# Gates of an expert layer: index selection in 16-bit floats, four heads at a time

## The chip, the cores and the metric

The kernel runs on one core of a Trainium2 chip, in one launch. The metric is device time in microseconds (us) from start to end of an execution. The engines are TensorE (PE, with PEld its weight loads), VectorE (DVE), ScalarE (ACT), GpSimd (POOL) and the DMA queues, of which SP's carries nearly all direct transfers and POOL's the indirect gathers.

## The reference, cut to what matters

The reference is a block with a gated linear recurrence, a convolution, an expert layer, and then two attention layers with their MLPs, all over 512 tokens of width 1024. The change is in the expert layer:

```python
def peer_layer(h, w_q, sub_keys, u_tab, v_tab):          # 512 tokens, 8 heads, 128 x 128 experts
    q = (hf @ w_q).reshape(T, 8, 2, 128)
    s = jnp.einsum('thpd,hpnd->thpn', q, sub_keys)       # two lists of 128 scores for each head
    sc, idx = lax.top_k(s, 16)
    cand = (sc[:, :, 0, :, None] + sc[:, :, 1, None, :]).reshape(T, 8, 256)
    cidx = (idx[:, :, 0, :, None] * 128 + idx[:, :, 1, None, :]).reshape(T, 8, 256)
    top_sc, pos = lax.top_k(cand, 16)
    eidx = jnp.take_along_axis(cidx, pos, axis=-1)       # 16 experts for each head and token
    gate = jax.nn.softmax(top_sc, axis=-1)
    act = jax.nn.gelu(jnp.einsum('thkd,td->thk', u_tab[eidx], hf), approximate=False)
    return jnp.einsum('thk,thkd->td', gate * act, v_tab[eidx])
```

The last two lines run in blocks of 128 tokens in the reference.

## The kernel before

The 512 tokens are four blocks of 128, one token to a partition. `stage_p` treats them in two ways. Block 0 gathers: for each of its 128 (head, choice) slots an indirect DMA fetches one row of `peer_u` for each token (`gu`, 512 KB, four buffers), VectorE makes the dot product with the token (`gather_dots`, L662), and later the rows of `peer_v` (`gv`) are fetched and summed with their weights (`gather_sums`, L677 and L679). Blocks 1 to 3 are dense: all 16384 experts are multiplied with 384 tokens, `peer_u` in 32 chunks of four units of 512 KB (`unit`: load `raw` in SP's queue, ScalarE rounds it to `whi` in L103, VectorE makes the rest `wlo` in L104; then three products for each step, L121 to L123), with GELU into `at`, which goes to DRAM. The gates become a dense array G (128 x 128 experts for each token): VectorE makes one-hot rows of 16 tokens at a time from the two indices (L735 to L738, 16-bit), TensorE multiplies them (L743, L744), ScalarE evicts into the tile `G` (32 tokens, one buffer), and SP writes it to DRAM as `g_d` (L749), four times for a block, 12 in all. The second part (`p2`) reads `at` and `g_d` back (`gt`), multiplies them to `w` (L600), splits `w` (ScalarE and L113) and multiplies it with `peer_v` (L610 to L612), chunk by chunk; it can't begin before all of G is there, since each chunk of `gt` takes a slice from all 12 writes.

The indices come from `route`. After the top-16 of the scores, `gates` runs once for each block, all on VectorE but for one exponential: 50 candidate sums for a head, their top 16 with positions `pos`, the softmax `g`, and then the selection, which turns a position among the candidates into the two indices. The candidates lie in 16 segments; `pcst[:, 0]` holds the segments' starts, `pcst[:, 1]` the lengths. For each head, over 16 choices x 16 segments: M is 1 where the position is at or behind the start; the row sum of M times D (differences of the first indices) is the first index `iv`; the row sum of M times the lengths, taken from the position, is the place in the segment `bb`; M is then 1 at that place, and the row sum of M times the second indices is `jv`. These are nine operations in a row, on one pair of tiles M and Q.

Block 0's indices become `eidx`, and only then the gathers can start. Blocks 1 to 3 go through `gates_t` (transposes on TensorE, 16-bit copies) to the one-hot rows. The tiles of `gates` have one buffer each.

The order of work on each engine is made by the framework's planner when the kernel is built: it goes through the program with a priority for each instruction (program order, and a higher one for the loads and splits of `unit`) and a simulated time, and takes what is ready. Each engine then executes its list in order. So `wlo`, dots, one-hot rows and gates are mixed on VectorE, and an edit of durations can change the order of all lists.

Of the kernel before, what the change touches and what calls it, by code (L numbers as in the profile page):

```python
# [9 lines left out]
F32 = mybir.dt.float32  # L10
F32R = mybir.dt.float32r
F16 = mybir.dt.float16
# [3 lines left out]
ALU = mybir.AluOpType  # L16
AX = mybir.AxisListType
# [3 lines left out]
P = 128  # L21
# [31 lines left out]
class Kern:  # L53
# [628 lines left out]
    def route(self, pq, X, g_d, gather):  # L682
        nc, tc, A = self.nc, self.tc, self.A
        with self.pool("p_rt") as pt:
            iota = pt.tile([P, P], F32, name="iota")
            nc.sync.dma_start(out=iota, in_=A["iota"])
            self.iota16 = iota[:, 0:16]
            pcst = pt.tile([P, 2, 16], F32, name="pcst")
            nc.sync.dma_start(out=pcst, in_=A["peer_cst"])
            v16 = [pt.tile([P, 16, 16], F32, name=f"v16_{b}") for b in range(4)]  # L690
            i16 = [pt.tile([P, 16, 16], U32, name=f"i16_{b}") for b in range(4)]
            with self.pool("p_route") as pr:
# [14 lines left out]
            with self.pool("p_gates") as pr:  # L707
# [8 lines left out]
                g, iv, jv = self.gates(pr, v16[0], i16[0], pcst)  # L716
# [7 lines left out]
                for b in range(1, 4):  # L724
                    gT, iT, jT = self.gates_t(pr, pq, *self.gates(pr, v16[b], i16[b], pcst))
                    for hf in range(4):
                        G = pr.tile([P, P, 32], F32, tag="G", name="G", bufs=1)
                        for c in range(2):
# [10 lines left out]
                            for t4 in range(4):  # L739
                                ps = pq.tile([P, T], F32, tag="G", name="Gp").rearrange("p (t i) -> p t i", t=4)  # L740
                                for tt in range(4):
# [5 lines left out]
                                    out=G[:, :, u0:u0 + 4], in_=ps.rearrange("p t i -> p i t"), func=AF.Copy, scale=2.0 ** -15)  # L747
# [11 lines left out]
    def gates(self, pr, v16, i16, pcst):  # L759
        nc = self.nc  # L760

        def t(tag, shape, dt=F32, bufs=1):
            return pr.tile([P] + shape, dt, tag=tag, name=tag, bufs=bufs)
        fi = t("fi", [16, 16])
        nc.vector.tensor_copy(out=fi, in_=i16)
        vv = v16.rearrange("p (h s) a -> p h s a", s=2)
        ff = fi.rearrange("p (h s) a -> p h s a", s=2)
        cand = t("cand", [8, NCAND])
        cand2 = t("cand2", [8, NCAND])
        for a in range(16):  # L770
            s0, n = STARTS[a], SEG[a]
            nc.vector.tensor_tensor(
                cand[:, :, s0:s0 + n], vv[:, :, 1, 0:n], vv[:, :, 0, a:a + 1].to_broadcast([P, 8, n]), ALU.add)
        top = t("top", [8, 16])
        pos = t("pos", [8, 16], U32)
        for h in range(8):
            self.top16(top[:, h], pos[:, h], cand[:, h], cand2[:, h])
        g = t("g", [8, 16])
        ssum = t("ssum", [8, 1])
        nc.vector.tensor_tensor(g, top, top[:, :, 0:1].to_broadcast([P, 8, 16]), ALU.subtract)  # L780
        nc.scalar.activation(out=g, in_=g, func=AF.Exp)
        nc.vector.tensor_reduce(out=ssum, in_=g, axis=AX.X, op=ALU.add)
        nc.vector.reciprocal(out=ssum, in_=ssum)
        nc.vector.tensor_tensor(g, g, ssum.to_broadcast([P, 8, 16]), ALU.mult)
        pf = t("pf", [8, 16])
        nc.vector.tensor_copy(out=pf, in_=pos)

        D = t("D", [8, 16])
        nc.vector.tensor_copy(out=D[:, :, 0:1], in_=ff[:, :, 0, 0:1])
        nc.vector.tensor_tensor(D[:, :, 1:16], ff[:, :, 0, 1:16], ff[:, :, 0, 0:15], ALU.subtract)  # L790
        iv, jv, bb = t("iv", [8, 16]), t("jv", [8, 16]), t("bb", [8, 16])
        M, Q = t("M", [16, 16]), t("Q", [16, 16])
        for h in range(8):
            def row(x):
                return x.unsqueeze(1).to_broadcast([P, 16, 16])

            def col(x):
                return x.unsqueeze(2).to_broadcast([P, 16, 16])
            nc.vector.tensor_tensor(M, col(pf[:, h]), row(pcst[:, 0]), ALU.is_ge)
            nc.vector.tensor_tensor(Q, M, row(D[:, h]), ALU.mult)  # L800
            nc.vector.tensor_reduce(out=iv[:, h], in_=Q, axis=AX.X, op=ALU.add)
            nc.vector.tensor_tensor(Q, M, row(pcst[:, 1]), ALU.mult)
            nc.vector.tensor_reduce(out=bb[:, h], in_=Q, axis=AX.X, op=ALU.add)
            nc.vector.tensor_tensor(bb[:, h], pf[:, h], bb[:, h], ALU.subtract)
            nc.vector.tensor_tensor(M, col(bb[:, h]), row(self.iota16), ALU.is_equal)
            nc.vector.tensor_tensor(Q, M, row(ff[:, h, 1]), ALU.mult)
            nc.vector.tensor_reduce(out=jv[:, h], in_=Q, axis=AX.X, op=ALU.add)
        return g, iv, jv

    def gates_t(self, pr, pq, g, iv, jv):  # L810
# [564 lines left out]
def pack(I):  # L1375
    I = {k: np.asarray(v) for k, v in I.items()}
    D = {}
    D["x"] = np.ascontiguousarray(I["x"][0].T.reshape(KD, P, T).transpose(1, 0, 2))
    vec = [
# [5 lines left out]
    ]  # L1385
    D["vec"] = np.ascontiguousarray(np.concatenate(vec, axis=1))
    D["c"] = I["c"]
# [50 lines left out]
```

## Time and profile before

| | us |
|---|---|
| median of 3 runs | 3200.18 (3192.09 to 3202.19) |
| the profiled execution, its own time | 3207.16 |
| its span, first to last instruction | 3205.2 |
| PE busy | 3065.3 (96%) |
| DVE busy | 2249.6 (70%) |
| ACT busy | 1243.2 (39%) |
| POOL busy | 415.1 (13%) |

The mean granted clock of TensorE is 0.979. `route` and the first part of the expert layer lie between about 640 and 1350 us of the span, the second part ends at about 1940. Times inside the span are counted from its first instruction. The shares are means over all stages; the rows further down are from the expert layer alone.

### The profile page before, as it was taken

The page shows a single profiled execution, that of the slowest core. Times are in us where ns is not written, and L with a number is a line of the kernel's source. Part 1 is how long each engine was busy: PE and PEld are TensorE (multiplying, and loading weights), DVE is VectorE, ACT ScalarE, POOL GpSimd, SP SyncE. Part 2 cuts the span into 40 slices and gives each one's busy share as a digit, 9 for nine tenths or more (in the row PEclk, how much of TensorE's full clock was granted, in tenths as well). Part 3 has the DMA queues.
Part 4 walks back from the last instruction along what each step waited for, and adds up shares of the span by engine and source line. Part 5 has one row for each costly group of instructions (what it writes and reads, how often), then busy time and mean ns, then how long its engine had stood idle before and what let it go on. Part 6 is the DMA issues. An engine that isn't in the chain of part 4 may idle for free.

```text
span 3205.2 us, 40593 instructions
## 1 busy us (share of the span) xinstructions
PE 3065.3 (96%) x15313; PEld 2592.2 (81%) x15313; DVE 2249.6 (70%) x4020; ACT 1243.2 (39%) x1963; POOL 415.1 (13%) x328
## 2 busy tenths in 40 slices
PE   5999999899999999798988999999999999999998
PEld 4778878789999999687777788678888877778886
DVE  7989977699899998577777655545544457554443
ACT  3257762334334343332222334553222245532221
POOL 0000000000334332034444101000000000000000
PEclk9999999999999999899999999999999999999999
DMA  6452227434899998798998753222333333133332
GB/s 219 143 168 72 68 85 250 153 98 158 303 336 362 325 361 332 249 361 321 353 335 321 284 170 93 61 66 81 105 99 93 110 92 96 51 96 97 97 99 72
DMA packets 199827, 579.71 MB, mean 181 GB/s; under 512 B 18288, under 2 KB 72448, under 8 KB 198096
## 3 DMA queue, kind: packets, MB, share of 16 engines
q1 hardware_dynamic: 159424, 431.36, 40.5%
q0 software_dynamic: 39776, 144.97, 12.1%
q8 instruction: 120, 1.97, 0.3%
q10 hardware_dynamic: 432, 0.80, 0.1%
q14 instruction: 75, 0.61, 0.1%
HBM read 525.34 MB, written 62.21 MB: 183 GB/s over the span
## 4 chain that ended last, share of the span: by engine, by line
PE 70%; DVE 10%; DMA 9%; issue 6%; ACT 2%; POOL 2%; SPq 0%; POOLq 0%; DVEq 0%; ACTq 0%
PE g L121 17%; PE g L122 17%; PE g L123 17%; DMA gv<-in_peer_v,eidx 3%; DVE wlo L104 2%; DMA raw<-in_peer_v 2%; DMA gu<-in_peer_ur,eidx 2%; DVE gu L662 2%; PE S L1245 1%; PE g L610 1%; PE ac L610 1%; PE g L611 1%; PE g L612 1%; PE ac L611 1%; PE ac L612 1%
## 5 line engine op out<-in xcount | busy, mean ns | idle before, releaser
L103 ACT CAST whi<-raw 128x1024 fp32r<-128x1024 f32 (+1 forms) x553 | 575.8, 1049 | 1203.5 <-PE g L122 667.1
L121 PE MATMUL g<-xh,whi 128*128 128x512 f32 (+1 forms) x2408 | 892.3, 372 | 17.8 <-ACT xh L112 8.9
L123 PE MATMUL g<-xh,wlo 128*128 128x512 f32 (+1 forms) x2408 | 891.4, 371 | 6.6 <-DVE wlo L104 6.6
L122 PE MATMUL g<-xl,whi 128*128 128x512 f32 (+1 forms) x2408 | 894.4, 372 | 3.4 <-DVE xl L113 3.4
L104 DVE TENSOR_TENSOR wlo<-raw,whi 128x1024 fp32r<-128x1024 f32 (+1 forms) x553 | 675.3, 1224 | 194.7 <-ACT whi L103 191.1
L121 PEld LDWEIGHTS g<-xh,whi 128*128 128x128 f32 x2408 | 456.2, 190 | 81.0 <-ACT xh L112 9.4
L123 PEld LDWEIGHTS g<-xh,wlo 128*128 128x128 f32 x2408 | 456.0, 189 | 63.7 <-DVE wlo L104 8.9
L122 PEld LDWEIGHTS g<-xl,whi 128*128 128x128 f32 x2408 | 456.0, 189 | 61.6 <-DVE xl L113 5.6
L653 POOL DMA_INDIRECT gv<-in_peer_v,eidx x128 | 197.0, 1539 | 352.7 <-DVE yt L679 240.7
L653 POOL DMA_INDIRECT gu<-in_peer_ur,eidx x128 | 161.6, 1263 | 475.8 <-DVE ga L662 226.6
L610 PE MATMUL g<-whi,wph 128*128 128x512 f32 x384 | 156.1, 408 | 52.6 <-ACT whi L103 37.2
L122 PE MATMUL g<-ml,whi 128*128 128x512 f32 x512 | 199.2, 389 | 0.0
L121 PE MATMUL g<-mh,whi 128*128 128x512 f32 x512 | 199.2, 389 | 0.0
L123 PE MATMUL g<-mh,wlo 128*128 128x512 f32 x512 | 199.2, 389 | 0.0
L188 POOL TENSOR_TENSOR tr_r<-tr_v,mhalf 128x4 f32<-128x4 f32 x15 | 16.4, 1094 | 1275.7 <-DVE tr_v L187 1275.7
L927 DVE TENSOR_TENSOR h<-g,h 128x512 f32<-128x512 f32 x64 | 44.3, 692 | 194.1 <-PE g L123 194.1
L679 DVE SCALAR_TENSOR_TENSOR yt<-gv,ga,yt 128x1024 f32<-128x1024 f32 x127 | 163.0, 1284 | 11.6 <-DMA gv<-in_peer_v,eidx 10.8
L327 DVE SCALAR_TENSOR_TENSOR s<-glu,vec,s 128x512 f32<-128x512 f32 x232 | 165.4, 752 | 0.1
L662 DVE CUSTOM_DVE_ANT_0 gu<-gu,xt 128x1024 f32<-128x1024 f32 x128 | 155.3, 1219 | 13.8 <-DMA gu<-in_peer_ur,eidx 13.7
L610 PE MATMUL ac<-whi,wph 128*128 128x512 f32 x384 | 157.5, 411 | 0.0
L611 PE MATMUL ac<-whi,wpl 128*128 128x512 f32 x384 | 156.6, 408 | 0.0
L611 PE MATMUL g<-whi,wpl 128*128 128x512 f32 x384 | 155.4, 405 | 0.0
(446 smaller groups left out, 4616.6 us busy)
## 6 DMA issues: line engine op xcount, KB each, us to landing
raw<-in_peer_u SPq DMA_DIRECT2D x128, 512.0 KB, 6.0
raw<-in_peer_v SPq DMA_DIRECT2D x128, 512.0 KB, 8.6
raw<-in_mlp_in SPq DMA_DIRECT2D x64, 512.0 KB, 3.6
raw<-in_mlp_out SPq DMA_DIRECT2D x64, 512.0 KB, 3.6
raw<-in_w_in SPq DMA_DIRECT2D x56, 512.0 KB, 3.6
g_d<-G SPq DMA_DIRECT2D x12, 2048.0 KB, 11.1
gt<-g_d SPq DMA_DIRECT2D x32, 768.0 KB, 8.8
act_d<-at SPq DMA_DIRECT2D x31, 768.0 KB, 7.3
```

Of the source, the lines that this page charges most:

```text
L103: nc.scalar.copy(out=hi[:, :n], in_=raw[:, :n])
L104: nc.vector.tensor_sub(out=lo[:, :n], in0=raw[:, :n], in1=hi[:, :n].bitcast(F32))
L121: nc.tensor.matmul(ps, wh, xh, start=start, stop=False)
L122: nc.tensor.matmul(ps, wh, xl, start=False, stop=False)
L123: nc.tensor.matmul(ps, wl, xh, start=False, stop=stop)
L327: nc.vector.scalar_tensor_tensor(o, glu[n][:, j:j + T], self.v("conv_w", n * 31 + j), acc, ALU.mult, ALU.add)
L610: nc.tensor.matmul(ps, wh[:, i], hi[:, s], start=first, stop=False)
L611: nc.tensor.matmul(ps, wl[:, i], hi[:, s], start=False, stop=False)
L612: nc.tensor.matmul(ps, wh[:, i], lo[:, s], start=False, stop=last)
L653: self.nc.gpsimd.indirect_dma_start(out=t, out_offset=None, in_=tab, in_offset=bass.IndirectOffsetOnAxis(ap=self.eidx[:, s:s + 1], axis=0))
L662: nc.vector.tensor_tensor_reduce(out=u, in0=u, in1=self.xt, scale=1.0, scalar=0.0, op0=ALU.mult, op1=ALU.add, accum_out=self.ga[:, s:s + 1])
L679: nc.vector.scalar_tensor_tensor(self.yt, v, self.ga[:, s:s + 1], self.yt, ALU.mult, ALU.add)
```

## The change

The selection works on four heads at a time (64 rows of choices in place of 16), so that nine operations for each of eight heads become nine for each of two halves. M, Q, the positions, D, the second indices, the place and the constants are 16-bit floats (all values are whole numbers up to 128); the sums `iv`, `bb`, `jv` stay fp32. Where a value repeats along a row it is stored twice in a row (`pf`, `b2`), so that the innermost dimension of every operand is a pair or longer. New are the copy `f1` for each block and two copies of constants at the start.

```diff
-            self.iota16 = iota[:, 0:16]
-            pcst = pt.tile([P, 2, 16], F32, name="pcst")
-            nc.sync.dma_start(out=pcst, in_=A["peer_cst"])
+            pc32 = pt.tile([P, 2, 16], F32, name="pc32")
+            nc.sync.dma_start(out=pc32, in_=A["peer_cst"])
+            pcst = pt.tile([P, 3, 16], F16, name="pcst")
+            nc.vector.tensor_copy(out=pcst[:, 0:2], in_=pc32)
+            nc.vector.tensor_copy(out=pcst[:, 2], in_=iota[:, 0:16])
...
-        pf = t("pf", [8, 16])
-        nc.vector.tensor_copy(out=pf, in_=pos)
-
-        D = t("D", [8, 16])
+
+
+        pf = t("pf", [8, 16, 2], F16)
+        nc.vector.tensor_copy(out=pf, in_=pos.unsqueeze(3).to_broadcast([P, 8, 16, 2]))
+
+        D = t("D", [8, 16], F16)
...
+        f1 = t("f1", [8, 16], F16)
+        nc.vector.tensor_copy(out=f1, in_=ff[:, :, 1])
         iv, jv, bb = t("iv", [8, 16]), t("jv", [8, 16]), t("bb", [8, 16])
-        M, Q = t("M", [16, 16]), t("Q", [16, 16])
-        for h in range(8):
...
+        b2 = t("b2", [8, 16, 2], F16)
+        M, Q = t("M", [64, 16], F16), t("Q", [64, 16], F16)
+
+        def pairs(x):
+            return x.rearrange("p n (a two) -> p n a two", two=2)
+
+        def col(x, h4):
+            return x[:, h4].rearrange("p h k two -> p (h k) two").unsqueeze(2).to_broadcast([P, 64, 8, 2])
+
+        def row(x):
+            return x.rearrange("p (a two) -> p a two", two=2).unsqueeze(1).to_broadcast([P, 64, 8, 2])
+
+        def heads(x):
+            return x.rearrange("p (h k) a -> p h k a", k=16)
+
+        def hrow(x, h4):
+            return x[:, h4].unsqueeze(2).to_broadcast([P, 4, 16, 16])
+
+        def total(out, h4):
+            nc.vector.tensor_reduce(out=out[:, h4], in_=heads(Q), axis=AX.X, op=ALU.add)
+        for h4 in (slice(0, 4), slice(4, 8)):
+            nc.vector.tensor_tensor(pairs(M), col(pf, h4), row(pcst[:, 0]), ALU.is_ge)
+            nc.vector.tensor_tensor(heads(Q), heads(M), hrow(D, h4), ALU.mult)
+            total(iv, h4)
+            nc.vector.tensor_tensor(pairs(Q), pairs(M), row(pcst[:, 1]), ALU.mult)
+            total(bb, h4)
+            nc.vector.tensor_tensor(b2[:, h4], pf[:, h4], bb[:, h4].unsqueeze(3).to_broadcast([P, 4, 16, 2]), ALU.subtract)
+            nc.vector.tensor_tensor(pairs(M), col(b2, h4), row(pcst[:, 2]), ALU.is_equal)
+            nc.vector.tensor_tensor(heads(Q), heads(M), hrow(f1, h4), ALU.mult)
+            total(jv, h4)
```

## Rows read from the trace of the kernel before

**Rows 1.** Stretches: length, busy time (instructions) of PE, PEld, DVE, ACT, POOL; PEclk, DMA share, GB/s.
```profile
818.00:1060.00 242.00, 241.08 (x1557) 237.61 (x1556) 229.35 (x429) 98.01 (x146) 93.24 (x76) 1.00 0.94 347
1060.00:1233.00 173.00, 166.79 (x1092) 161.33 (x1091) 163.74 (x262) 67.25 (x105) 59.94 (x48) 0.97 0.94 347
1233.00:1321.00 88.00, 85.39 (x617) 82.35 (x616) 68.27 (x70) 40.28 (x66) 13.84 (x9) 0.98 0.77 270
1321.00:1348.00 27.00, 5.64 (x49) 5.37 (x49) 4.67 (x5) 6.50 (x10) 0.00 (x0) 0.65 0.63 231
...
1400.00:1800.00 400.00, 361.50 (x1478) 290.92 (x1477) 297.49 (x233) 114.75 (x104) 164.72 (x107) 0.94 0.90 329
```

**Rows 2.** Chain of waits, 1314 to 1356 us: start, length, what.
```profile
1317.55 8.77 DMA g_d<-G
...
1333.00 6.27 DMA g_d<-G
1339.34 4.90 DMA gt<-g_d
1344.33 1.77 DVE w L600
...
1347.64 1.65 PE g L610 x3
...
1350.57 0.43 PE g L611
...
1355.07 0.23 PE g L612
```

**Rows 3.** Timeline of ACT at the last `peer_u` unit: start, length, instruction.
```profile
1320.88 0.48 ACT L581 ACTIVATE at<-g 128x384 f32<-128x384 f32 x1
```

**Rows 4.** Timeline of SP's queue: writes of `g_d`, last of block 1 to first of block 3.
```profile
1047.11 0.87 SPq L749 DMA_DIRECT2D g_d<-G  x1
...
1119.15 0.33 SPq L749 DMA_DIRECT2D g_d<-G  x1
...
1201.35 0.85 SPq L749 DMA_DIRECT2D g_d<-G  x1
...
1269.17 0.42 SPq L749 DMA_DIRECT2D g_d<-G  x1
```

**Rows 5.** Timeline of DVE: steps among other work; last steps of blocks 2 and 3.
```profile
842.69 1.21 DVE L104 TENSOR_TENSOR wlo<-raw,whi 128x1024 fp32r<-128x1024 f32 x1
843.83 0.41 DVE L801 TENSOR_REDUCE iv<-Q 128x16 f32<-128x256 f32 x1
844.16 1.21 DVE L662 CUSTOM_DVE_ANT_0 gu<-gu,xt 128x1024 f32<-128x1024 f32 x1
...
1074.81 0.42 DVE L807 TENSOR_REDUCE jv<-Q 128x16 f32<-128x256 f32 x1
...
1229.11 0.41 DVE L807 TENSOR_REDUCE jv<-Q 128x16 f32<-128x256 f32 x1
```

**Rows 6.** Groups on DVE, 700 to 1480 us: instruction and count | busy us, mean ns | idle before.
```profile
L104 DVE TENSOR_TENSOR wlo<-raw,whi 128x1024 fp32r<-128x1024 f32 x159 | 194.4, 1225 | 30.1 <-ACT whi L103 29.6 <-PE Gp L744 0.4
...
L735 DVE TENSOR_TENSOR oj<-io,jT 128x2048 f16<-128x2048 f16 x24 | 29.0, 1220 | 0.0
...
L799 DVE TENSOR_TENSOR M<-pf,pcst 128x256 f32<-128x256 f32 x32 | 13.9, 433 | 0.0
...
L802 DVE TENSOR_TENSOR Q<-M,pcst 128x256 f32<-128x256 f32 x32 | 13.4, 419 | 0.4
L803 DVE TENSOR_REDUCE bb<-Q 128x16 f32<-128x256 f32 x32 | 13.3, 414 | 0.5
...
L804 DVE TENSOR_TENSOR bb<-pf,bb 128x16 f32<-128x16 f32 x32 | 5.5, 171 | 0.4
```

**Rows 7.** Instructions on the tile `gv`: duration min/median/max ns, first and last start.
```profile
L679 DVE SCALAR_TENSOR_TENSOR yt<-gv,ga,yt x127: 1269/1280/1322, 1351.6 to 1814.7; 128x1024 f32<-128x1024 f32 x127
```

**Rows 8.** Waits of POOL, 740 to 1262 us: total us, times, longest.
```profile
POOL gu L653 <- DVE ga L662: 226.6, 97, 7.3
```

More of the change, by code (lines that the diff above doesn't have):

```diff
@@ L791, in gates @@
+        nc.vector.tensor_copy(out=f1, in_=ff[:, :, 1])
         iv, jv, bb = t("iv", [8, 16]), t("jv", [8, 16]), t("bb", [8, 16])
-        M, Q = t("M", [16, 16]), t("Q", [16, 16])
-        for h in range(8):
[L794 to L807, printed above, removed]
+        b2 = t("b2", [8, 16, 2], F16)
```

## The prediction

> **What bounds the kernel now.** I read four views in this order: the stretches, to see which engine is full where the gates run; the chain of waits at the end of that stage; the queues and timelines, to see what makes that end late; the groups of instructions, for the prices.
>
> The stretches [rows 1] show the expert layer's first part. From 818 to 1321 us three things are full at once: TensorE (241.08 of 242 us, 166.79 of 173, 85.39 of 88), VectorE (95% until 1233 us, 78% after) and the DMA engines (share 0.94, then 0.77). TensorE does the dense products with `peer_u` and, in between, the small one-hot products that build G. It can't go faster, so taking work from VectorE is worth only what TensorE now waits for. In the three stretches that is 0.92 + 6.21 + 2.61 = 9.7 us. The large hole comes next: from 1321 to 1348 us TensorE works 5.64 of 27 us, and the granted clock is 0.65 on the mean: after some 6 us of standing still it goes from the upper of its two levels (2.4 GHz) to the lower (1.2 GHz).
>
> The chain of waits [rows 2] says who makes this hole. The last `peer_u` unit is evicted at 1320.88 us [rows 3], but the last quarter of G of the last token block waits until the quarter before it has left its only buffer (1317.55 + 8.77 us); then it is built, goes to DRAM (6.27), comes back as `gt` (4.90), is multiplied and split, and TensorE starts the second part at 1347.64. Its first products take 0.43 us each, against 0.23 at 1355 us, back at the upper level.
>
> Why is G late? The `g_d` writes in the SP queue [rows 4]: the four of block 2 go from 1119.15 to 1201.35, 27 us apart, but between the last of block 1 (1047.11) and the first of block 2 there are 72 us, and between the last of block 2 and the first of block 3 (1269.17) 68. The holes are gates: those of block 2 end at 1074.81 and those of block 3 at 1229.11 [rows 5], each about 28 us after the previous block's last `g_d`. And the gates are slow because each of their operations depends on the one before: the same rows show the planner putting a `wlo` of 1.21 us or a dot (L662) of 1.21 us between one operation and the next. From 842.69 to 844.16 a `wlo` and one selection step of 0.41 us together take a turn of 1.5 us, and a dot follows. A block has 72 such steps, 9 for each of 8 heads.
>
> **The change, part by part.** Durations are from [rows 6].
>
> Removed, for each head: five operations of 128x256 at 419 to 433 ns (L799, L800, L802, L805, L806), three reductions at 414, one subtraction at 171. That is 2.11 + 1.24 + 0.17 = 3.53 us; times 8 heads, times 4 blocks: 113 us.
>
> Added, for each half of four heads: five operations of 128x1024 in 16 bits. L735, whose operands are in pairs and 16 bits wide as here, does 2048 elements in the 1220 ns that L104 needs for 1024 in fp32. So 1024 in pairs cost what 512 cost in fp32; between 256 (420 ns) and 1024 (1225 ns) the slope is 1.05 ns an element, so 0.69 us. Three reductions of 1024: no row has one in 16 bits. Bounds: 1.22 us at the fp32 rate (a reduction of 256 costs 414 ns, as much as a product of 256), 0.69 at the pairs' rate; I take 1.22, because the reductions of before are the nearest rows. The subtraction now writes 128 values with one fp32 input: 0.29 by the same slope. Sum 5 x 0.69 + 3 x 1.22 + 0.29 = 7.4 us, 59 for eight halves. The copy `f1`, a `pf` twice as long and the constants add about 0.3 us a block: 61 in all. The Trainium skill (VectorE: DVE Perf Modes, "The perf-mode tier table") gives tensor_reduce one element a cycle whatever its type; by it the reductions stay at the price that I took, and by the other bound the sum would be 48. No run so far shows a 16-bit reduction.
>
> So VectorE is relieved of 113 - 61 = 52 us. Independent instructions overlap by some 0.1 us each (843.83 to 844.16 is a step of 0.33 for 0.41), and 288 instructions become 72: without the overlaps the relief is 113 - 29 - (61 - 7) = 30 us. Bounds 30 to 52. If the 16-bit operations ran at one element a cycle (1.22 instead of 0.69), they would be 9 to 31.
>
> More than the sum, the number of turns falls: 72 steps in a row become 18. At one filler of 1.2 us a step, the fillers between fall from about 86 to 22 us a block, with the fillers run after instead.
>
> What it moves: the gates of block 0 end earlier, so the gathers begin earlier; the gates of blocks 2 and 3 fit into the 80 us in which the block before builds its G. If they do, both holes of [rows 4] close to the pace of 27 us: 72 - 27 and 68 - 27, together 86 us, and the last `g_d`, now at 1333, comes at 1247. The VectorE sum alone would allow 30 to 52. What is needed is less: for `gt` to be there when the last `peer_u` unit is evicted (1321.4) the last G must go out by 1310, 23 us earlier. So either figure covers it, with little to spare at the lower end.
>
> What then sets the end is TensorE: its `peer_u` products until 1321.4, later by the G products that now run alone in the hole (5.64 us at about half clock, so 2.8 at full), then the unchanged way from `w` to the first product (1344.33 to 1347.64: 3.3 us). Start of the second part: 1321.4 + 2.8 + 3.3 = 1327.5 in place of 1347.64: **20 us**. The first twelve products, 0.43 in place of 0.23: **2.5 us**. The 9.7 us of TensorE's waits in the first part: bounds from all of it gained to 35 lost (below); I take nothing.
>
> The dots also end earlier, and the sums over gathered `peer_v` rows can begin before the hole: now they stand in VectorE's order behind the first `w`, 127 of them from 1351.6 to 1814.7 us, 3.65 us each [rows 7]. In the second part the sums and the other loads fill the DMA engines, and TensorE works only 361.50 of 400 us [rows 1]. That is 9.6% lost, so each sum moved out spares about 0.35 us. At most 24 fit into the 88 us from 1233 to 1321: 8 us. I take **3**, since the planner may leave them where they are.
>
> Sum: 20 + 2.5 + 3 = 25.5 us, some 26. The profiled execution took 3207.2 us (span 3205.2 and 2 around it), so 3181. It lay 7 us over the median of the runs (3200.2): in runs as shown, **3174 us**. Whatever is less than 0.3% (9.6 us) a measurement of this kernel can't tell from no change.
>
> **The rivals.**
>
> *The hole stays (no change).* The planner orders all engines anew, and G could still be the last to come: its quarter has one buffer and goes at 24 to 28 us each, and freed turns may go to dots and not to gates (POOL waited 226.6 us for dots to give back their buffers [rows 8], so there is appetite). For it: the gates come in program order behind the previous block's G. Against it: even the relief by the sum is over 23 us. Then at most the waits of the first part go: 0 to 9.7 us, a median of 3190 to 3200.
>
> *The gathers take the DMA engines (slower).* Dots now wait for VectorE; if it is freed, gathers go as fast as the DMA engines let them, at a share of 0.94 already, and the `peer_u` loads come late, behind `g_d` writes in SP's queue too. The price is that of the second part, where TensorE loses 38.5 of 400 us: 9.6% in place of the 1.9% of 818 to 1321; over these 503 us 39 lost against 25.5 gained, so 13 us slower: 3213. It decides from a loss of 5% more than now on. Against it: the bytes are the same, and after the dots the DMA share is only 0.77, so what is lost early is partly regained.
>
> *More than the hole (faster).* The 9.7 us of waits go too, and the sums start well before: 20 + 2.5 + 9.7 + 8 = 40: 3160.
>
> *The 16-bit form doesn't pay.* At one element a cycle the relief is 9 to 31 us. The turns still fall to a quarter, so about half the hole goes: 13 us, 3187. L735 speaks against it; only `heads`/`hrow`, where one operand repeats in rows of 16, has no row.
>
> **How the numbers follow.** Forecast 0.57, more than the hole 0.12, 16 bits not paying 0.04, hole stays 0.14, gathers slower 0.13. The likeliest gives 3174 (its own range 3164 to 3186: the sums at 8 us and half of the waits, or none of the sums and half of the hole's fall). To leave out no more than 2 in 10 the range goes from 3148 (the larger gain, and 12 us for what a new order of all engines can bring where TensorE waits later, some 38 us from 1400 to 1800) to 3204 (the hole stays). Faster 0.73, the same 0.14, slower 0.13.
>
> **What would show it.** Groups: the 16-bit operations at about 0.69 us and the reductions at 1.22, eight for each place in the code. Timeline: gates of block 3 done by about 1200 and not 1229; first gather earlier than now. SP queue: last `g_d` well before 1310. Stretches: the hole of 27 us down to some 4, granted clock full through it. Wrong, if the last `g_d` still comes after the last `peer_u` eviction, if TensorE waits for `raw` in the first part more than 20 us, or if the second part grows by what the first gave.

## The result, and the profile after

Six runs of the changed kernel have a median of 3182.43 us (3177.39 to 3187.97), six of the kernel before 3201.81. That is 19 us less by the medians; the ratio is 0.9946, 95% interval 0.9932 to 0.9961, which is 17 us (12 to 22). The time is inside the stated range and moved in the forecast direction, 8 us above the forecast of 3174. The profiled execution has a span of 3184.4 us in place of 3205.2.

The groups on VectorE come first, for the prices of the new operations (as [rows 6]).

```profile
L104 DVE TENSOR_TENSOR wlo<-raw,whi 128x1024 fp32r<-128x1024 f32 x159 | 193.6, 1219 | 62.6 <-ACT whi L103 62.5
...
L817 DVE TENSOR_REDUCE iv<-Q 128x64 f32<-128x1024 f16 x8 | 9.7, 1217 | 0.0
...
L820 DVE TENSOR_TENSOR Q<-M,D 128x1024 f16<-128x1024 f16 x8 | 5.5, 687 | 0.0
...
L824 DVE TENSOR_TENSOR b<-pf,bb 128x128 f16<-128x128 f16 x8 | 2.3, 287 | 0.0
```

A 16-bit operation of 1024 takes 0.69 us, also with the operand that repeats in rows of 16 (L820); a reduction of as many takes 1.22. Before `wlo`, VectorE now stands idle 62.5 us for ScalarE in place of 29.6: it has slack where it had little.

SP's queue shows the writes of `g_d` (as [rows 4]; here the last of blocks 1 and 2, the first of the next, and the very last).

```profile
1002.00 0.33 SPq L751 DMA_DIRECT2D g_d<-G  x1
1032.11 0.33 SPq L751 DMA_DIRECT2D g_d<-G  x1
...
1111.32 0.33 SPq L751 DMA_DIRECT2D g_d<-G  x1
1133.28 0.33 SPq L751 DMA_DIRECT2D g_d<-G  x1
...
1205.19 0.33 SPq L751 DMA_DIRECT2D g_d<-G  x1
```

The gaps between blocks are 30 and 22 us, about as long as those inside a block (19 to 30), and the last write is issued at 1205 in place of 1333. G is ready 120 us before it is wanted. The stretches show what that did (as [rows 1], divided at the new end of the first part).

```profile
818.00:1060.00 242.00, 236.67 (x1595) 229.94 (x1595) 230.61 (x330) 99.03 (x155) 94.90 (x67) 0.99 0.93 338
1060.00:1233.00 173.00, 166.63 (x1180) 158.85 (x1179) 146.64 (x178) 74.08 (x118) 72.30 (x46) 0.99 0.96 364
1233.00:1329.00 96.00, 95.67 (x552) 95.35 (x551) 58.93 (x62) 32.76 (x47) 39.09 (x29) 1.00 0.95 343
1329.00:1333.00 4.00, 0.03 (x1) 0.03 (x1) 4.00 (x4) 2.68 (x4) 2.92 (x2) 1.00 0.98 354
1333.00:1338.00 5.00, 4.95 (x14) 3.49 (x15) 5.00 (x4) 1.82 (x2) 2.21 (x1) 0.66 0.91 323
1400.00:1800.00 400.00, 368.07 (x1548) 298.06 (x1547) 286.68 (x224) 119.57 (x108) 140.00 (x90) 0.97 0.88 322
```

The hole of 27 us is one of 4. But even these 4 us bring the granted clock down after them: 0.66 from 1333 to 1338. And the second part, at 368 of 400 us, still stands idle for 8%. The next two views, the products of the second part and TensorE's waits in it, say how long it is and why. In each, the lines of the kernel before come first.

```profile
L610 PE MATMUL g<-whi,wph x384: 387/389/794, 1347.6 to 1931.4; 128*128 128x512 f32 x192
L610 PE MATMUL ac<-whi,wph x384: 389/389/632, 1349.1 to 1937.5; 128*128 128x512 f32 x192
...
L610 PE MATMUL g<-whi,wph x384: 387/389/717, 1333.0 to 1909.1; 128*128 128x512 f32 x192
L610 PE MATMUL ac<-whi,wph x384: 389/389/632, 1333.9 to 1915.3; 128*128 128x512 f32 x192
```

```profile
PE g L610 <- ACT whi L103: 37.2, 15, 3.8
...
PE g L610 <- ACT whi L103: 37.0, 17, 4.8
```

From the first to the last product start there are 582.3 us (before: 589.9), of which 37 are waits for `whi`, ScalarE's rounded copy of the weights. ScalarE in its turn waits in this part for `raw`, the weight load, more than for anything else:

```profile
ACT whi L103 <- DMA raw<-in_peer_v: 168.3, 58, 10.1
```

### The profile page after: what moved, and what is told of

Its sections match the earlier page's. It is cut to its first block, busy times and chain, and to the rows that moved or that the text cites. A ratio compares the mean times of both kernels' runs of the same rounds, so it can differ in the third digit from the quotient of the medians.

```text
span 3184.4 us, 40396 instructions
## 1 busy us (share of the span) xinstructions
PE 3059.4 (96%) x15313; PEld 2583.7 (81%) x15313; DVE 2203.8 (69%) x3810; ACT 1243.6 (39%) x1963; POOL 442.5 (14%) x328
## 4 chain that ended last, share of the span: by engine, by line
PE 75%; DMA 7%; DVE 7%; issue 6%; ACT 3%; POOL 2%; POOLq 0%; DVEq 0%; SPq 0%; ACTq 0%
PE g L121 18%; PE g L122 18%; PE g L123 18%; DMA raw<-in_peer_v 4%; PE g L610 2%; PE g L611 2%; PE ac L610 2%; PE ac L611 2%; PE g L612 2%; PE ac L612 2%; DVE wlo L104 1%; PE S L1265 1%; POOL gu L653 1%; DMA raw<-in_peer_u 1%; DMA gv<-in_peer_v,eidx 1%
## 5 line engine op out<-in xcount | busy, mean ns | idle before, releaser
L104 DVE TENSOR_TENSOR wlo<-raw,whi 128x1024 fp32r<-128x1024 f32 (+1 forms) x553 | 673.9, 1220 | 245.0 <-ACT whi L103 241.9
L122 PEld LDWEIGHTS g<-xl,whi 128*128 128x128 f32 x2408 | 455.6, 189 | 62.5 <-issue 5.9
L653 POOL DMA_INDIRECT gu<-in_peer_ur,eidx x128 | 188.8, 1475 | 448.4 <-DVE ga L662 231.1
L662 DVE CUSTOM_DVE_ANT_0 gu<-gu,xt 128x1024 f32<-128x1024 f32 x128 | 154.6, 1218 | 15.1 <-DMA gu<-in_peer_ur,eidx 15.1
```

Source lines behind the costliest of these rows:

```text
L104: nc.vector.tensor_sub(out=lo[:, :n], in0=raw[:, :n], in1=hi[:, :n].bitcast(F32))
L122: nc.tensor.matmul(ps, wh, xl, start=False, stop=False)
L653: self.nc.gpsimd.indirect_dma_start(out=t, out_offset=None, in_=tab, in_offset=bass.IndirectOffsetOnAxis(ap=self.eidx[:, s:s + 1], axis=0))
L662: nc.vector.tensor_tensor_reduce(out=u, in0=u, in1=self.xt, scale=1.0, scalar=0.0, op0=ALU.mult, op1=ALU.add, accum_out=self.ga[:, s:s + 1])
```

## The experiments

Theory A, formed from the result: the gates end late because their many dependent steps each wait behind a filler, so the number of steps decides. Theory B: the sum of VectorE work decides. After the first four runs neither explained the times, and theory C took their place: the hole closes as soon as G is in time, and what remains is TensorE waiting for late loads, which changes with the order of all lists. Theory D gives the gain to block 0's early gathers. Theories E and F are two causes for the late loads.

All runs in one table. "Last `g_d`" is its issue, "end" the last eviction (`at`) of the first part, "start" and "length" the products of the second part from first to last start, "waits" TensorE's for `whi` there; all in us, from one profiled execution each. The ratio is against the kernel before on the same chip.

| run | ratio (95%) | last `g_d` | end | start | length | waits |
|---|---|---|---|---|---|---|
| before, first profile | | 1333.0 | 1320.9 | 1347.6 | 589.9 | 37.2 |
| before, once more | | 1330.0 | 1317.7 | 1344.6 | 580.2 | 34.8 |
| the change | 0.9946 (0.9932 to 0.9961) | 1205.2 | 1328.7 | 1333.0 | 582.3 | 37.0 |
| two heads, fp32 | 0.9963 (0.9947 to 0.9979) | 1295.4 | 1330.1 | 1334.0 | 586.6 | 34.9 |
| one head, 16 bits | 0.9934 (0.9917 to 0.9951) | 1299.5 | 1327.0 | 1330.9 | 574.7 | 31.6 |
| four heads, one rate | 0.9995 (0.9981 to 1.0009) | 1259.0 | 1335.2 | 1339.5 | 592.2 | 40.4 |
| before, gates first | 0.9956 (0.9940 to 0.9972) | 1335.2 | 1332.4 | 1350.6 | 568.7 | 28.8 |
| block 0 only | 0.9944 (0.9931 to 0.9957) | 1314.9 | 1326.6 | 1333.4 | 579.0 | 32.2 |
| blocks 1 to 3 only | 0.9933 (0.9920 to 0.9947) | 1228.5 | 1323.9 | 1327.7 | 569.6 | 27.7 |
| sums held | 0.9958 (0.9943 to 0.9972) | 1206.0 | 1328.4 | 1333.2 | 576.2 | 29.7 |
| the change, gates first | 0.9927 (0.9913 to 0.9941) | 1201.9 | 1321.7 | 1325.5 | 579.2 | 31.4 |
| three gather buffers | 0.9834 (0.9820 to 0.9849) | 1205.9 | 1328.3 | 1332.9 | 553.5 | 16.5 |
| more raw buffers | 0.9784 (0.9770 to 0.9798) | 1203.6 | 1326.9 | 1332.2 | 524.4 | none |
| before, more raw buffers | 0.9815 (0.9799 to 0.9831) | 1325.7 | 1319.8 | 1342.9 | 523.6 | none |

**Two heads in fp32** (36 steps a block).

```diff
-        M, Q = t("M", [16, 16]), t("Q", [16, 16])
-        for h in range(8):
+        M, Q = t("M", [2, 16, 16]), t("Q", [2, 16, 16])
+        for h in [slice(i, i + 2) for i in range(0, 8, 2)]:
...
```

> Two heads at a time, all in fp32: 36 steps a block in place of 72, 16-bit floats nowhere. By the rates of before a step of 512 elements costs 0.69 us, so a block's selection is 4 x (8 x 0.69 + 0.2) = 23 us against 28: VectorE is relieved of about 21 us over four blocks. Theory A (the number of dependent steps among fillers sets when the gates end): the last write of G moves from 1333 us by 50 us or more, the hole between the parts is gone, 13 to 20 us faster than before. Theory B (what counts is the sum of VectorE work taken away): the last write moves by about 20 us, the hole shrinks by half, 5 to 10 us faster.

**One head in 16 bits** (72 steps).

```diff
-        M, Q = t("M", [64, 16], F16), t("Q", [64, 16], F16)
+        M, Q = t("M", [16, 16], F16), t("Q", [16, 16], F16)
...
-        for h4 in (slice(0, 4), slice(4, 8)):
+        for h4 in [slice(h, h + 1) for h in range(8)]:
...
```

> One head at a time as before, but in 16 bits and pairs: still 72 steps a block. Five operations of 256 at 0.29 us, three reductions at 0.41, a subtraction: 8 x (1.45 + 1.24 + 0.18) = 23 us a block against 28, the same relief of some 20 us as the run with two heads in fp32. Theory A (steps): the last write of G moves by 10 to 25 us only, 0 to 10 us faster than before, and clearly less than two heads in fp32. Theory B (sum): the same as two heads in fp32.

The groups of these two kernels, one line each of five and three, give VectorE's work.

```profile
L803 DVE TENSOR_TENSOR Q<-M,D 128x512 f32<-128x512 f32 x16 | 11.0, 686 | 0.1
...
L804 DVE TENSOR_REDUCE iv<-Q 128x32 f32<-128x512 f32 x16 | 10.9, 679 | 0.1
```

```profile
L817 DVE TENSOR_REDUCE jv<-Q 128x16 f32<-128x256 f16 x32 | 13.3, 415 | 0.5
...
L826 DVE TENSOR_TENSOR Q<-M,f 128x256 f16<-128x256 f16 x32 | 9.3, 289 | 0.5
```

Two heads in fp32 come to 90 us over four blocks, one head in 16 bits to 92, against 113: the same relief, with half the steps or all of them. The last write of G moved by 38 and 34 us, so theory A fell: steps don't decide, the sum does. By the sum of the groups the four forms rank as their last writes do (92 us: 1299; 90: 1295; four heads at one rate 80: 1259; the change 59: 1205). Each us of relief moved the write by 1.6 to 2.4 us; a likely reason, not tested, is that the gates get only a part of VectorE. But the times don't follow: by the ratios one head in 16 bits is 9 us faster than its twin with the same relief and G equally in time (their intervals just overlap), and theory B's gains (5 to 10 us) fit neither.

**Four heads, one element a cycle.** The constants, D and the second indices stay fp32.

```diff
-            pcst = pt.tile([P, 3, 16], F16, name="pcst")
+            pcst = pt.tile([P, 3, 16], F32, name="pcst")
...
-        D = t("D", [8, 16], F16)
+        D = t("D", [8, 16])
...
-            nc.vector.tensor_tensor(heads(Q), heads(M), hrow(f1, h4), ALU.mult)
+            nc.vector.tensor_tensor(heads(Q), heads(M), hrow(ff[:, :, 1], h4), ALU.mult)
```

> The change as it is (18 steps a block), but the second operands (constants, D, second indices) stay fp32, so that the operations on them should take 1.22 us in place of 0.69. VectorE's relief falls from 52 to some 32 us. Theory A: as the changed kernel, 17 to 21 us faster than before, last write of G within 30 us of 1205. Theory B: the last write moves by some 32 us, to about 1300, and the gain is a third less, 10 to 15 us.

One fp32 operand is enough: all five operations took 1.22 us.

```profile
L818 DVE TENSOR_TENSOR Q<-M,D 128x1024 f16<-128x1024 f16 x8 | 9.7, 1215 | 0.0
```

(The view gives one input type only; D is fp32 here.) The last write, at 1259, fits neither theory A (within 30 us of 1205) nor theory B (about 1300). G was in time by 76 us, the hole closed, and the gain is nothing (0.9995). TensorE's waits in the first and the second part of this run:

```profile
PE g L121 <- ACT whi L103: 15.1, 8, 4.7
```

```profile
PE g L610 <- ACT whi L103: 40.4, 16, 5.8
```

Late loads cost 15.1 us in the first part (4.7 before) and 40.4 in the second (37.2). The first part ended 14 us later than before, so that the second began only 8 us earlier, and it was as long as the longest of the others (592.2). It looks like the rival in which the gathers take the DMA engines, but the gathers did not go faster here: the dots lasted from 811 to 1285 us, 474 in place of 436, and POOL waited 228 us for them (227 before). Why the loads were late in this order stays open.

**The kernel before, gates first.**

```diff
-                    gT, iT, jT = self.gates_t(pr, pq, *self.gates(pr, v16[b], i16[b], pcst))
+                    with self.tc.high_priority(offset=20000):
+                        gts = self.gates(pr, v16[b], i16[b], pcst)
+                    gT, iT, jT = self.gates_t(pr, pq, *gts)
```

> The kernel before with its fp32 one-head gates, only that the planner takes the gates of blocks 1 to 3 ahead of dots and one-hot rows (not ahead of the units' loads and splits). No operation is changed, VectorE's work is the same. Theory A (G is late because the gates' steps wait behind fillers): the last write of G moves by 60 us or more and most of the gain of the change is here too, 10 to 18 us faster than before. Theory B: nothing moves but the order, within 5 us of before.

Theory A has the gain right and its reason wrong: G was as late as before (1335) and the second part began 3 us later. (The hole itself is 18 us, only because the first part ended 12 us later.) Theory B misses the gain. The kernel is 14 us faster (0.9956), and its second part takes 568.7 us, with 28.8 us of waits. No work was removed at all. So an edit that only reorders is worth as much as most of the change, and a total alone says little of a cause here.

**Block 0 only, and blocks 1 to 3 only** (the other blocks call the selection of before).

```diff
+                    gT, iT, jT = self.gates_t(pr, pq, *self.gates_old(pr, v16[b], i16[b], pc32))
```

> The new selection for block 0 only; blocks 1 to 3 keep one head in fp32. VectorE's relief is a quarter, some 13 us. Theory C (the hole closes, worth about 14 us at the start of the second part, when the last write of G is out before some 1310; the rest is TensorE waiting for late weight loads, which changes with the order of all lists): the last write moves by 10 to 20 us, the second part starts at 1335 to 1345, and the gain is 3 to 12 us. Theory D (the early gathers of block 0 make the gain): 15 us or more here.

```diff
+                g, iv, jv = self.gates_old(pr, v16[0], i16[0], pc32)
```

> The new selection for blocks 1 to 3 only; block 0, whose indices start the gathers, keeps one head in fp32. Theory C: gathers begin as late as before (first dot at 820 to 824), last write of G before 1270, second part starts at 1330 to 1336; 10 to 22 us faster. Theory D: at most 5 us faster.

Block 0 alone moves the last write by 18 us, and that already closes most of the hole (start 1333.4): the 23 us that the prediction asked for were not quite needed. Its total (18 us faster) is above theory C's 12 and by itself what theory D asked for. With blocks 1 to 3 alone the dots begin as late as before (825.7) and the kernel is 21 us faster, where theory D allowed 5, so theory D fell. Either part of the change gains as much as the whole, so the gains don't add up: once G is in time, the rest of the relief moves the start by little (1333.4, 1327.7, and 1333.0 with all of it).

**Sums held.**

```diff
+                nc.vector.scalar_tensor_tensor(self.ga, last[:, 3, 0:P], 0.0, self.ga, ALU.mult, ALU.add)
```

> The changed kernel, with one small operation on the weights of the gathered rows that reads the last dense activations, so that the sums over gathered rows can't start before the end of the first part (the output is the same). The changed kernel starts them 60 us before that. If the early sums are worth what was forecast (3 us, at most 8): the second part gets 3 to 10 us longer, its waits for weight loads last until about 1790 in place of 1732; the first part ends up to 5 us earlier, since fewer gathers run beside its last loads. In all 0 to 8 us slower than the changed kernel, 12 to 19 us faster than before. If the sums' place is of no account: as the changed kernel.

The first sum moved from 1273 to 1332 us, and in the profiled execution the second part got 6 us shorter, not longer. By the ratios the kernel is 4 us slower than the changed one, as forecast for sums that are worth 3 us, but the intervals overlap. These runs can't tell 3 us from nothing.

**The change, gates first** (the edit of above on the changed kernel).

> The changed kernel, with the gates of blocks 1 to 3 ahead in the planner. G is in time already, so by the hole nothing is left to gain: second part at 1329 to 1336 us, as in the changed kernel. By theory C the total still moves by up to 10 us either way, all of it in TensorE's waits for weight loads and in the granted clock after them; if the gates' lateness were still of weight, it is 5 us or more faster.

G was no earlier (1202), the start 7 us earlier (1325.5, before the 1329 that was forecast), the total 6 us lower with intervals that overlap. Theory C allows it, within its 10 us, and so does the other reading (5 us or more); the run doesn't separate them.

**More buffers for the loads, and fewer for the gathers.** Every other unit of the second part takes its `raw` from a pool of two more; in the other run the gathered rows have three buffers.

```diff
+            self.rn += 1
+            wr = self.rx if self.rx is not None and self.rn % 2 else self.wr
-            raw = self.wr.tile([P, 1024], F32, tag="raw", name="raw")
+            raw = wr.tile([P, 1024], F32, tag="raw", name="raw")
...
-            with self.pool("p2") as pp, self.pool("p2p", space=PSUM) as pv:
+            with self.pool("p2") as pp, self.pool("p2r", bufs=2) as rx, self.pool("p2p", space=PSUM) as pv:
+                self.rx = rx
...
```

> The changed kernel, with two more buffers for weight loads in the second part (five in place of three; every other unit takes one of the two). Theory E (the second part loses time because single loads are late beside gathers, and three buffers don't bridge it): TensorE's waits for loads there fall from 37 us to under 15, the granted clock stays near 1.00, the second part falls from 582 us to 540 to 560; 20 to 40 us faster than the changed kernel. Theory F (the DMA engines are simply full while the sums run): the waits stay at 28 to 40 us, the second part at 570 to 590, or the sums end later in exchange.

```diff
-            v = self.gather_rows(pool.tile([P, 1024], F32, tag="gv", name="gv", bufs=4), tab, s)
+            v = self.gather_rows(pool.tile([P, 1024], F32, tag="gv", name="gv", bufs=3), tab, s)
```

> The changed kernel, with three buffers in place of four for the gathered rows of the second part, so that fewer gathers run beside the weight loads. Theory E: the sums go slower (end 40 us or more later than 1732), but the single waits get shorter, the clock stays up, and the second part gets shorter by 5 to 15 us. Theory F: the waits are spread over a longer time, the second part is the same within 5 us.

The stretches of the run with more buffers:

```profile
1350.00:1500.00 150.00, 150.00 (x663) 124.23 (x662) 115.14 (x90) 50.61 (x46) 61.20 (x36) 1.00 0.96 351
1500.00:1650.00 150.00, 150.00 (x663) 124.20 (x663) 119.89 (x93) 51.70 (x47) 61.31 (x37) 1.00 0.96 354
1650.00:1800.00 150.00, 150.00 (x664) 124.20 (x663) 117.16 (x91) 50.72 (x46) 49.72 (x30) 1.00 0.92 335
```

TensorE is busy in all of it, at the upper clock, beside sums that still run to 1784 us. The second part takes 524.4 us and the kernel 3126.36 us, 56 less than the changed kernel and 70 less than before: theory E, with more than its 20 to 40 us. So the DMA engines were not simply full (F): at a share of 0.96 they deliver in time if the next loads have been asked for earlier. ScalarE's waits for `raw` in the second part fell from 168 to 48 us. The wait itself was 37 us of the 58 that went; for the other 21 TensorE was busy, 545.3 us for products that took 524.4 here, at a granted clock of 0.97 on the mean in place of 0.99. Three gather buffers do half of it from the other side: waits 16.5 us, 29 us less in the second part (more than the 5 to 15 expected), the sums later by 85 us.

**The kernel before once more, and with more buffers.**

> The kernel before once more, for the spread of its parts from execution to execution. If the order of the lists alone sets the second part, it is again 585 to 595 us long with 36 to 38 us of waits for loads; if executions differ, it lies elsewhere in 570 to 595, while the hole of 27 us before it is the same within 1 us.

The hole is the same (26.9 us from end to start, 26.7 at first), the second part 580.2 us in place of 589.9: two executions of one program differ there by 9.7 us, more than the 7.6 between the first profiles of before and of the change. The start differs too, by 3 us (1347.6 and 1344.6).

> The kernel before (one head in fp32) with the two more buffers for weight loads in the second part. With the second part at the pace of its products in both, what is left between this and the changed kernel with the same buffers (3126 us) is the worth of the change without the scatter of late loads. If the change's worth is the hole and its slow clock: last write of G again at about 1330, hole of 26 to 28 us, second part 525 to 530 us long from 1345 to 1348, in all 3140 to 3146 us, 14 to 20 us over 3126. If most of the measured 19 us of the change came from elsewhere in the second part: under 8 us over it.

With no waits for loads in the second part of either, the kernel before takes 3136.44 us and the changed one 3126.36. **The change is then worth some 10 us**, less than the 14 to 20 expected; by the intervals of the two ratios it is 3 to 17. The products of the second part, first in the kernel before and then in the changed one, both with the two buffers, show where the 10 us are:

```profile
L614 PE MATMUL g<-whi,wph x384: 389/389/792, 1342.9 to 1860.4; 128*128 128x512 f32 x192
...
L614 PE MATMUL g<-whi,wph x384: 389/389/794, 1332.2 to 1850.5; 128*128 128x512 f32 x192
```

The starts differ by 10.7, the second parts by less than 1. The last write of G is also 7 us earlier in this kernel than in the first profile of before, so its hole is 23 us.

## Why the prediction came out as it did

The direction, the place and the mechanism are right: the hole was G being late, it closed, and the start of the second part moved with it. What was mis-sized is the largest term, the 20 us by which the second part was to start earlier: it measured 14.6 between the two profiles, 11.6 against the other execution of before, and 10.7 between the two kernels with more buffers. Against the first profile, what is missing is the first part's later end (below). The other two are smaller still because the start of the kernel before scatters, and the forecast was made from the latest of three (1347.6, 1344.6, 1342.9). By its steps:

- **Prices.** Forecast 0.69, 1.22 and 0.29 us; measured 0.687, 1.21 to 1.22 and 0.287. The sum of the selection is 59 us as forecast. The value taken for the 16-bit reduction was the right end. The Trainium skill (VectorE: DVE Perf Modes, "The perf-mode tier table") lists the reduction at one element a cycle for every type; with 1217 ns for 1024 16-bit elements, as much as an fp32 operation of 1024 takes in L104 (1219), this trace agrees.
- **G in time.** Forecast 1247, or some 30 to 50 us earlier by the sum alone; measured 1205. The argument of the turns was wrong as a cause (one head in 16 bits has all 72 steps and moves the last write about as far as two heads in fp32, 34 and 38 us); what the sum is worth was undersized.
- **The end of the first part.** Forecast 1321.4 + 2.8 = 1324.2, measured 1329.2 (last eviction 1328.7 and its length): 5 us late. One step that failed here is "the constants add about 0.3 us a block", a price with no wait. VectorE's timeline at the start of `route`:

```profile
608.62 1.23 DVE L104 TENSOR_TENSOR wlo<-raw,whi 128x1024 fp32r<-128x1024 f32 x1
611.23 0.18 DVE L691 CAST pcst<-iota 128x16 f16<-128x16 f32 x1 [1.38 <-DMA iota<-in_iota]
611.44 0.18 DVE L690 CAST pcst<-pc 128x32 f16<-128x32 f32 x1
611.53 1.22 DVE L104 TENSOR_TENSOR wlo<-raw,whi 128x1024 fp32r<-128x1024 f32 x1
612.67 0.68 DVE L171 TENSOR_TENSOR acc<-acc,tmp 128x512 f32<-128x512 f32 x1
```

The copies of the constants wait 1.38 us for a small DMA, and queued behind them on VectorE is the sum of squares `acc`, for which TensorE waits:

```profile
PE m L179 <- DVE acc L171: 4.0, 1, 4.0
...
PE m L179 <- DVE acc L171: 5.8, 1, 5.8
```

The first line is from the kernel before, the second from the changed one. The wait is 4.0 in every kernel without these copies (five profiles) and 5.7 to 6.5 in every one with them (nine). That is 1.8 us. The first product on the sub-keys in `route` (L701 before, L703 after) starts 2.9 us later, at 640.6. In "before, gates first", which has no copies, it starts at 641.4, but that execution was already 3 us late before this point: counted from the previous `acc`, the first sub-key product comes after 30.9 to 31.7 us in the five profiles without the copies and after 32.7 to 34.3 in the nine with them. So some 2 us are put down to the copies. Another 1.9 are in the first part's own waits, 11.6 us in place of 9.7; that is within the scatter, since the first parts of the two executions of before end 3.2 us apart. The last 1 us stays open. Moving the copies behind the norm wasn't tried.
- **The slow clock.** 2.5 us were counted, and the clock was to stay full, since the forecast had seen it fall in a stop of some 6 us. But behind the stop of 4 us the granted clock was 0.66 as well, and 14 products took 4.95 us from 1333 on. At most 1 us of the 2.5 came (an estimate: 5 us at 0.66, against some 5.4 at 0.50 in the kernel before).
- **The early sums.** 3 us were counted. The sums began 78 us earlier; whether that gained anything the run that held them back can't tell.
- **The second part.** It was forecast to shift; it came out 7.6 us shorter between the two profiles, without a cause in the change that the runs show: it lies between 568.7 and 592.2 us in ten orders, and 9.7 us apart in two executions of one. That this makes up for what was missed above is luck: 14.6 earlier start, 7.6 shorter, 1.4 lost behind, 20.8 in all between the two profiles.

So of the 17 to 19 us some 10 are the mechanism that was forecast, shown by the start of the second part. The rest lies in the second part, where the order of the lists and the execution scatter by as much; no run ties it to the change, and the interval of the 17 us (12 to 22) overlaps that of the 10 us (3 to 17). The rival that loses to the gathers did not come: in the changed kernel the dots lasted 455 us in place of 436 and POOL waited 231 us for them, so the freed time of VectorE didn't make the gathers go faster. Late loads in the first part took 15.1 us in four heads at one rate, but there too the dots were slower, not faster.

## What to carry to other kernels

When a planner orders all engines anew, a total of a per cent is no proof of a mechanism: read the places where the edit can act (here the last write of G and the start of the second part), and remove the noisiest wait in both versions before comparing. Relief of a full engine is worth only what is late behind it, and beyond that nothing: in these runs 18 us earlier was nearly enough, and 128 us earlier gave little more. And a copy of 0.2 us that is loaded by a DMA can stand in an in-order list ahead of what the whole chain waits for, so ask of each added operation what it waits for and who is queued behind it.

## What was not expected of the hardware

Waits of TensorE cost more than their length: over the 524.4 us of the undisturbed second part, the changed kernel's 37 us of waits went with 58, and the 28.8 us of "before, gates first" with 44. Over the twelve profiles with waits it is 1.5 to 1.8 times the waits and the mean granted clock of the second part was 0.95 to 0.98, where it was 0.99 and 1.00 in the two without. After a stop of only 4 us the granted clock was 0.66 over the next 5. At a DMA share of 0.96 and 351 GB/s the loads were still in time with five buffers, where at 0.92 and 338 GB/s with three (1350 to 1500 us of the first profile of before) TensorE stood idle 9 of 150 us.
